# A two-layer hybrid encoder: calls recorded and ordered before they are issued, grouped q, k and v projected with tokens on rows, values 512 wide

## The chip, the cores and the metric

The kernel runs on one core of one Trainium2 chip. The time is device microseconds of one execution; the result is a median of several. Engines: TensorE (PE) multiplies, VectorE (DVE), ScalarE (ACT) and GpSimd (POOL) do the elementwise work, SyncE (SP) issues most transfers.

## The reference

512 tokens of width 1024 in f32 pass two layers. `@` is a matrix product, every norm is an RMS norm, all residuals are plain sums:

```python
h = rms_norm(x, g_mix)
na_q, na_k, na_v, g_q, g_k, g_v = split(h @ w_in)      # 512, 512, 512, 512, 128, 128 columns
a = neighbourhood_attention(na_q, na_k, na_v, rpb)     # 8 heads of 64; 128 queries see 256 keys each here
g_q = rope(rms_norm(g_q per head, q_norm))             # 8 query heads of 64
g_k = rope(rms_norm(g_k per head, k_norm))             # 2 key heads: 4 query heads share one
b = softmax(g_q @ g_k.T / 8) @ g_v                     # all 512 keys, in blocks of 128 queries
x = x + concat(a, b) @ w_out
x = x + memory_attention(rms_norm(x), rms_norm(mem))   # 4 heads of 128 over 256 memory tokens
u = conv3(rms_norm(x) @ w_up)                          # width-3 depthwise over positions
x = x + (silu(gate half of u) * value half of u) @ w_down
```

A last norm follows the second layer.

## The kernel before, in words

**Numbers.** Each f32 operand is split into a high part (`hi`) and a low part (`lo`) of a reduced f32 format. A product is three matmuls, high with high, high with low, low with high (`mm3`), so 1024 rows make 8 x 3 = 24 matmuls per output tile. Only some small jobs (statistics, spreading a row over partitions) are plain f32 matmuls.

**Layout.** Activations are held transposed: `xT` is 8 tiles of 128 features by 512 tokens, and `xg` the split, scaled operand. The projection for neighbourhood attention gives q and k transposed (pairs of heads, 128 rows by 512 tokens) and v with tokens on rows (4 blocks of 128 tokens, twice 256 columns). The grouped projection gives six transposed tiles of 128 x 512: k, q of four head pairs, and v, which is transposed back to tokens on rows.

**Grouped q and k (`gqa_rope`).** VectorE multiplies the tile in two ways with the rotation's table (lines 1147 and 1148), ScalarE squares it (1149), four transfers inside the chip swap its rows for the rotation, matmuls with `pairs` sum the squares over each head's 64 rows, GpSimd takes the power -1/2, matmuls with `ident` spread the result back over the rows, and VectorE multiplies it in (1180) and splits it. `late(n, ...)` holds each of these steps back by some TensorE time.

**Keys doubled.** `split_k` writes a head's key parts on 64 partitions; `double` (line 976) copies them with SP to the other 64, as the score matmul contracts over high and low queries at once.

**Weights.** SP loads each weight block (`raw`, 512 KB, two buffers), ScalarE casts its high part (line 550), GpSimd or VectorE subtracts the low one (551); four buffers of each hold them.

**Attention.** `weave` runs the units of an attention as a pipeline: scores, softmax, transposes of the probabilities, values. Between its steps the `Filler` puts other projection work (the rest of the input projection, then the output projection, memory keys and values) until a quantum of TensorE time is used up (`NA_FILL`, `GQA_FILL`). Neighbourhood attention has 8 units, grouped attention 16 (128 queries of one pair of heads). Probabilities of two query blocks and both heads of the pair share one `xg` tile; there are two such tiles. PSUM has 4 `mm`, 2 `sc` and 2 `tr` buffers.

**Order.** The program is written through `Counted` engines; buffers open in the written order, with priorities from `behind(n)`. At the end `put_in_order` lists the built instructions, prices them with formulas (`busy_and_length`, `HANDOVER`, `BYTES_PER_NS`, `LANDING`), runs them through a planner for six settings (`PLANS`), and fixes the best found order on each engine.

Of the kernel before, what the change touches and what calls it, by code (L numbers as in the profile page):

```python
# [11 lines left out]
F32 = mybir.dt.float32  # L12
# [7 lines left out]
P = 128  # L20
# [20 lines left out]
NA_ORDER = [("q", 0), ("k", 0), ("q", 1), ("k", 1), ("v", 0), ("q", 2), ("k", 2), ("q", 3), ("k", 3), ("v", 1)]  # L41
# [4 lines left out]
GQA_ORDER = ["k", 0, 1, "v", 2, 3]  # L46

NA_FILL = 2550
GQA_FILL = [2300] * 16 + [4300, 3600, 3000, 3000]
# [3 lines left out]
W_BEHIND, N_RAW, N_W, AHEAD, AHEAD_HELD, N_WARM, N_LATE, N_FIRST = 45, 2, 4, 2, 5, 6, 4, (7, 16)  # L53


class InOrder:


    def __init__(self, tc, engine):
        self.tc, self.engine = tc, engine  # L60

    def __getattr__(self, name):
        op = getattr(self.engine, name)
        return op


class Counted(InOrder):


    ns = 0.0  # L70

    def matmul(self, out, lhsT, rhs, **k):
        n = 1
        for d in rhs.shape[1:]:
            n *= d
        self.ns += max(107.0, (n + 32) / 2.4)
        return self.engine.matmul(out, lhsT, rhs, **k)  # L77


class Free:  # L80


    def __init__(self, engine):
        self.engine = engine

    def __getattr__(self, name):
        return getattr(self.engine, name)
# [74 lines left out]
def weave(n, steps, filler, quanta):  # L162
# [12 lines left out]
ENGINES = ["PE", "Activation", "DVE", "Pool", "SP"]  # L175
E_PE, E_ACT, E_DVE, E_POOL, E_SP = range(5)
PLANS = [
    ((60.0, 300.0, 300.0, 300.0, 0.0), 300, given, margin) for given in ((), (E_SP,)) for margin in (0.0, 40.0, 80.0)
]

HANDOVER, BYTES_PER_NS, LANDING = 40.0, 280.0, 2000.0


class Step:


    __slots__ = ("i", "ins", "engine", "busy", "length", "moved", "inside", "shared", "needs", "frees", "opens", "tiles")


def columns(ap):  # L190
    n = 1
    for _, c in ap.ap[1:]:
        n *= c
    return n


def tag_of(tensor):
    return re.sub(r"(_\d+)+$", "", tensor.name)


IN_PSUM = ("mm", "sc", "tr")


def busy_and_length(ins, kind, engine, reads, writes):

    n = max(columns(a) for a in (writes if engine == E_PE else reads + writes))
    if engine == E_PE:
        busy = max(110.0, (n + 32) / 2.4)
        if reads[0].dtype == F32 and not ins.is_transpose:
            busy = 312.0 if n > 64 else 222.0  # L210
        return busy, busy + 170.0
    narrow = min(a.ap[0][1] for a in writes) < P
    if engine == E_ACT:
        busy = 68.0 + 0.805 * n if any(tag_of(a.tensor) in IN_PSUM for a in reads) else 85.0 + 0.855 * n
        busy += 105.0 * (n > 1) * sum(columns(a) == 1 for a in reads) + 93.0 * (len(writes) > 1)
        return busy + 110.0 * narrow, busy + 105.0 + 100.0 * (len(writes) > 1)
    wide = sum(columns(a) > 16 for a in reads)
    if engine == E_DVE:
        if kind == "InstCustomDveAnt":
            return 382.0, 540.0  # L220
        busy = 64.0 + 1.05 * n
        if n <= 16:
            busy = 130.0
        elif kind == "InstTensorScalarPtr":
            busy = 120.0 + 1.05 * n if wide > 1 else 64.0 + 0.78 * n
        return busy + 100.0 * (narrow and n > 16), busy + 85.0
    if kind in ("InstTensorScalarPtr", "InstTensorCopy"):
        busy = 245.0 + 0.82 * n
    else:
        busy = 480.0 + 145.0 * n if n <= 8 else 120.0 + 2.2 * n  # L230
    return busy, busy + 45.0


class Course:


    def __init__(self, tc):
        self.bufs = {tag: m.bufs for p in tc.info.pools for tag, m in p.tag_meta.items()}
        self.steps, self.tag, self.users, self.opened = [], {}, {}, {}
        written, read = {}, {}  # L240
        for ins in tc.nc.cur_bb.bb.instructions:
            kind = type(ins).__name__
            if kind == "BassTilePoolBoundary":
                continue
            s = Step()
            s.i, s.ins, s.engine = len(self.steps), ins, ENGINES.index(str(ins.engine).split(".")[-1])
            s.needs, s.frees, s.opens, s.tiles, s.moved, s.inside = set(), set(), [], [], 0, False
            reads = [x.bass_ap for x in ins.ins if getattr(x, "bass_ap", None) is not None]
            writes = [x.bass_ap for x in ins.outs if getattr(x, "bass_ap", None) is not None]
            if kind == "InstDMACopy":  # L250
                s.busy = s.length = 450.0
                s.moved = 4
                for _, c in writes[0].ap:
                    s.moved *= c
                s.inside = all(type(a.tensor).__name__ == "Tile" for a in reads + writes)
            elif kind == "InstRegisterMove":
                s.busy = s.length = 50.0
            else:
# [1437 lines left out]
```

## Time and profile before

| | |
|---|---|
| median of 3 runs | 1368.02 us (1365.55 to 1368.59) |
| the profiled execution | 1366.98 us, its span 1365.2 |
| PE busy | 1345.2 us (99%), 7068 matmuls |
| DVE busy | 909.3 us (67%) |
| ACT busy | 680.0 us (50%) |
| POOL busy | 695.4 us (51%) |
| transfers | 139.88 MB, mean 102 GB/s |
| mean granted TensorE clock | 0.995 |

The span runs from the first to the last instruction; the time of the execution lies a little above it. An engine's busy time is the sum of what it has in work, so an engine at 99% still says nothing of how well each matmul is used. A group row of the profile gives its line and engine, output and inputs by name, shape and count, then the busy time and mean ns of one, then the idle time just before it with what ended it. The plain f32 matmuls appear twice each, since they take two passes. Roughly, neighbourhood attention of layer 0 ends and the grouped projection runs from 112 to 162 us, grouped attention from there to about 250 us, and the feed-forward network from some 340 us to 686; layer 1 follows in the same way.

### The profile page before, as it was taken

What the parts mean: (1) busy time and instruction counts of PE and PEld (TensorE: products, weight loads), DVE (VectorE), ACT (ScalarE), POOL (GpSimd) and SP (SyncE); (2) the same over time, 40 slices, a digit from 0 to 9 for tenths busy, and PEclk for the clock granted to TensorE, in tenths of its full rate; (3) what the DMA queues carried; (4) which work ended last, traced back from release to release, by engine and by line L of the source; (5) the groups of instructions that cost most, each with busy time, mean ns of one, the idle gap of its engine ahead of it and who ended that gap; (6) DMA issues with size and microseconds to landing.
All of it is one profiled execution on the core that took longest, in us unless ns stands there. A gap on an engine that the chain in (4) does not pass through costs nothing.

```text
span 1365.2 us, 19258 instructions
## 1 busy us (share of the span) xinstructions
PE 1345.2 (99%) x7068; PEld 1154.7 (85%) x7068; DVE 909.3 (67%) x1540; ACT 680.0 (50%) x1258; POOL 695.4 (51%) x493
## 2 busy tenths in 40 slices
PE   9899999999999999999999999999999999999997
PEld 7797889888888888888888988998888888888897
DVE  5567776565897188458546678746759934872884
ACT  5676577564443134234456767755644423432441
POOL 2467656736444444444643676657364444444451
PEclk9999999999999999999999999999999999999999
DMA  6745212322333333332345641133233333323331
GB/s 214 208 135 137 72 39 90 90 82 62 108 100 101 93 94 92 108 93 86 100 146 167 175 116 54 48 94 109 62 93 99 102 93 93 101 84 108 94 91 63
DMA packets 219358, 139.88 MB, mean 102 GB/s; under 512 B 6144, under 2 KB 212224, under 8 KB 219264
## 3 DMA queue, kind: packets, MB, share of 16 engines
q1 hardware_dynamic: 218160, 137.99, 34.4%
q8 instruction: 56, 0.92, 0.3%
q10 hardware_dynamic: 1104, 0.66, 0.2%
q14 instruction: 38, 0.31, 0.1%
HBM read 126.05 MB, written 2.10 MB: 94 GB/s over the span
## 4 chain that ended last, share of the span: by engine, by line
PE 94%; DVE 2%; DMA 1%; ACT 1%; issue 1%; POOL 1%; SPq 0%; ACTq 0%; DVEq 0%; POOLq 0%
PE mm L77 83%; PE sc L77 6%; PE tr L1228 2%; PE tr L77 1%; PE tr L1071 1%; DMA raw<-in_w_in 1%; PE tr L1418 1%; POOL lo L551 0%; DMA t<-t 0%; DVE r L818 0%; DMA par<-in_par 0%; ACT r L984 0%; ACT hi L550 0%; ACT r L966 0%; DVE r L766 0%
## 5 line engine op out<-in xcount | busy, mean ns | idle before, releaser
L551 POOL TENSOR_TENSOR lo<-raw,hi 128x1024 fp32r<-128x1024 f32 (+2 forms) x268 | 504.9, 1894 | 510.2 <-ACT hi L550 510.1
L77 PE MATMUL mm<-xg,hi 128*128 128x512 f32 x1920 | 597.2, 392 | 1.7 <-ACT t L1149 1.7
L77 PEld LDWEIGHTS mm<-xg,hi 128*128 128x128 f32 x1920 | 356.8, 188 | 72.9 <-ACT t L1149 1.9
L550 ACT CAST hi<-raw 128x512 fp32r<-128x512 f32 (+2 forms) x276 | 225.8, 837 | 302.3 <-PE mm L77 232.2
L77 PE MATMUL mm<-xg,lo 128*128 128x512 f32 x960 | 374.5, 390 | 0.0
L77 PE MATMUL mm<-r,hi 128*128 128x512 f32 (+1 forms) x1144 | 332.0, 373 | 0.0
L1519 DVE SCALAR_TENSOR_TENSOR t<-t,par,t 128x504 f32<-128x504 f32 (+1 forms) x352 | 287.7, 859 | 18.7 <-ACT t L1512 15.8
L77 PEld LDWEIGHTS mm<-r,hi 128*128 128x128 f32 x1144 | 207.3, 189 | 35.8
L77 PE MATMUL mm<-r,lo 128*128 128x512 f32 (+1 forms) x572 | 212.8, 372 | 0.0
L77 PEld LDWEIGHTS mm<-xg,lo 128*128 128x128 f32 x960 | 180.7, 188 | 37.9
L77 PEld LDWEIGHTS mm<-r,lo 128*128 128x128 f32 x572 | 107.8, 188 | 18.8
L772 POOL TENSOR_SCALAR t<-t,s 128x512 f32<-128x512 f32 (+1 forms) x112 | 66.7, 611 | 72.8 <-DVE s L1213 39.6
L1504 DVE TENSOR_TENSOR t<-mm,rep 128x512 f32<-128x512 f32 x88 | 60.3, 687 | 62.2 <-PE mm L77 47.0
L1548 DVE TENSOR_TENSOR xT<-xT,mm 128x512 f32<-128x512 f32 x32 | 22.0, 687 | 98.9 <-PE mm L77 98.9
L77 PE MATMUL sc<-r,r 128*128 128x256 f32 (+1 forms) x352 | 72.6, 334 | 0.3 <-DVE r L972 0.3
L1512 ACT ACTIVATE t<-t,par 128x512 f32<-128x512 f32 x88 | 67.5, 807 | 2.9 <-DVE t L1504 2.7
L77 PE MATMUL mm<-r,r 128*128 128x256 f32 (+1 forms) x428 | 64.7, 298 | 3.6 <-DVE r L766 2.6
L1524 ACT CAST r<-t 128x512 fp32r<-128x512 f32 x44 | 27.3, 620 | 78.4 <-DVE t L1522 78.4
L77 PEld LDWEIGHTS mm<-r,r 128*128 128x128 f32 x428 | 57.3, 191 | 6.9 <-DVE r L766 3.2
L1525 DVE TENSOR_TENSOR r<-t,r 128x512 fp32r<-128x512 f32 x44 | 48.1, 1092 | 17.2 <-ACT r L1524 16.5
L77 PEld LDWEIGHTS sc<-r,r 128*128 128x128 f32 x352 | 52.1, 190 | 5.3 <-ACT t L1049 0.4
L1205 DVE TENSOR_REDUCE s<-sc 128x1 f32<-128x512 f32 x64 | 43.5, 686 | 19.0 <-PE sc L77 18.9
(158 smaller groups left out, 1589.0 us busy)
## 6 DMA issues: line engine op xcount, KB each, us to landing
raw<-in_w_up SPq DMA_DIRECT2D x88, 512.0 KB, 3.6
raw<-in_w_in SPq DMA_DIRECT2D x33, 512.0 KB, 4.3
raw<-in_w_down SPq DMA_DIRECT2D x32, 448.0 KB, 3.5
raw<-in_w_mem_kv SPq DMA_DIRECT2D x16, 512.0 KB, 3.5
raw<-in_w_down SPq DMA_DIRECT2D x16, 512.0 KB, 3.8
r<-in_bias SPq DMA_DIRECT2D x16, 384.0 KB, 5.4
r<-r SPq DMA_DIRECT2D x22, 256.0 KB, 5.4
raw<-in_w_out SPq DMA_DIRECT2D x8, 512.0 KB, 3.6
```

The source lines that it names most:

```text
L77: return self.engine.matmul(out, lhsT, rhs, **k)
L550: act.copy(hi[:, k], raw[:, k])
L551: (POOL if eng[0] == "P" else DVE).tensor_sub(lo[:, k], raw[:, k], f(hi)[:, k])
L772: eng.tensor_scalar(e, e, sums[:, col : col + 1], 1.0, op0=ALU.mult, op1=ALU.mult)
L1205: DVE.tensor_reduce(nmx[:, c], sc[j], axis=AX.X, op=ALU.max, negate=True)
L1228: PE.transpose(tr[:, k * P : (k + 1) * P], es[j][:, k * P : (k + 1) * P], ident)
L1504: DVE.tensor_mul(u, us[side], ffn.rep)
L1512: ACT.activation(cc, u, AF.Identity, bias=par[:, l, CB + ch : CB + ch + 1], scale=w[1])
L1519: DVE.scalar_tensor_tensor(cc[:, dst], u[:, src], wi, cc[:, dst], op0=ALU.mult, op1=ALU.add)
L1524: ACT.copy(acts[j][0], cs[0])
L1525: DVE.tensor_sub(acts[j][1], cs[0], f(acts[j][0]))
L1548: DVE.tensor_add(xT[m], xT[m], pm)
```

## The change

**Calls are written down first.** The engines become `Taped` ones: each call makes a `Step` on a `Tape`, with what it reads and writes, and nothing is issued. At the end `Tape.plan` orders all steps with a planner of the same kind, and `play` issues them in that order. Buffers now open in the planned order, not in the written one. `behind` is gone. The planner's constants change (`LANDING` 1450 for 2000, `BYTES_PER_NS` 230 for 280, at most 8 transfers in flight), and transfers inside the chip have no price of their own any more.

**Grouped q, k, v with tokens on rows.** `gqa_project_kv` makes k and v of 128 tokens in one group of 24 matmuls, 256 wide; `gqa_project_q` all 8 heads of 128 tokens in one group of 24 matmuls, 512 wide. The norm is then a sum along a row (`head_norm`), the rotation two products with swapped halves, one product and one sum on VectorE (`turned`), and the result is transposed (4 transposes for k, 16 for q in a layer). k is scaled by its norm on GpSimd; q's norm enters the softmax instead, as a factor of the maximum and as the scale of the exponential (`gr`). The transfers that swapped rows and the matmuls with `pairs` and with `ident` (of a `t` tile) are gone.

**512 wide.** The v of neighbourhood attention and the memory values are projected 512 wide from four weight blocks of 2 x 128 rows (`plan_wide`, `get_wide`). The grouped values take all four query blocks of a pair at once, 512 wide, with one `xg` tile for each head of the pair.

**Smaller things.** `double` and `straddle` are called at once and placed by the planner. A loop before grouped attention finishes all q projections. The filler's quanta are smaller, and more work is done ahead (`N_FIRST`).

The core of the diff:

```diff
-W_BEHIND, N_RAW, N_W, AHEAD, AHEAD_HELD, N_WARM, N_LATE, N_FIRST = 45, 2, 4, 2, 5, 6, 4, (7, 16)
+N_RAW, N_W, AHEAD, AHEAD_HELD, N_WARM, N_LATE, N_FIRST = 2, 4, 2, 5, 6, 4, (12, 22)
...
-NA_FILL = 2550
-GQA_FILL = [2300] * 16 + [4300, 3600, 3000, 3000]
+NA_FILL = 2050
+GQA_FILL = [1850] * 16 + [3450, 2900, 2400, 2400]
...
-HANDOVER, BYTES_PER_NS, LANDING = 40.0, 280.0, 2000.0
+HANDOVER, BYTES_PER_NS, LANDING, IN_FLIGHT = 40.0, 230.0, 1450.0, 8
+ASIDE = {"mm": 1, "r": 9, "t": 9, "s": 9}
+PLANS = [((60.0, 300.0, 300.0, 300.0, 0.0), 300, margin, ASIDE, 3) for margin in (40.0, 80.0, 120.0)]
...
+class Tape:
...
+    def take(self, engine, name, call, args, kwargs):
+        s = Step(len(self.steps), engine, name, call, args, kwargs)
...
+    def play(self, tc):
...
+        for i in self.plan():
+            call, args, kwargs = self.steps[i].call
+            call(*args, **kwargs)
+            while n < len(issued):
+                if type(issued[n]).__name__ != "BassTilePoolBoundary":
+                    if issued[n].engine in last:
+                        tc.add_manual_dep(issued[n], last[issued[n].engine], follows, reason="planned")
+                    last[issued[n].engine] = issued[n].name
+                n += 1
...
@@ split_k
-                late(2, double)
+                double()
...
+        def turned(x, n, which, b, out):
...
+            halves = [slice(0, 32), slice(32, 64)]
+            for d, o in (halves, halves[::-1]):
+                DVE.tensor_mul(at(t2, o), at(x, d), table(1, d))
+            DVE.tensor_mul(x, x, table(0, slice(0, HD)))
+            DVE.tensor_add(out, x, t2)
+
+        def head_norm(x, n, which, b):
...
+            ACT.activation(sq, x, AF.Square)
...
+            DVE.tensor_reduce(view(v), sq, axis=AX.X, op=ALU.add)
...
+            POOL.tensor_tensor(r, v, mhalf[:, :n], op=ALU.pow)
+            return r
...
+        def gqa_project_q():
+
+            w = get_wide("gq")
+            for b in range(NB):
+                pm = ps_mm()
+                bs = slice(b * P, b * P + P)
+                for k in range(KC):
+                    wh, wl = (v[:, k % 2, :] for v in w[k // 2])
+                    mm3(pm, xg[k][0][:, bs], xg[k][1][:, bs], wh, wl, k == 0, k == KC - 1)
...
+                gr[b] = head_norm(x, 8, 0, b)
+                tq = tmp()
+                turned(x, 8, 0, b, tq.rearrange("p (h d) -> p h d", d=HD))
+                late(1.5, lambda b=b, tq=tq: gqa_turn_q(b, tq))
...
@@ gqa_scores
                 DVE.tensor_reduce(nmx[:, c], sc[j], axis=AX.X, op=ALU.max, negate=True)
+                DVE.tensor_mul(nmx[:, c], nmx[:, c], gr[b][:, h])
                 e = tmp()
-                ACT.activation(e, sc[j], AF.Exp, bias=nmx[:, c], accum_out=sums[:, c])
+                ACT.activation(e, sc[j], AF.Exp, bias=nmx[:, c], scale=gr[b][:, h], accum_out=sums[:, c])
...
@@ gqa_transpose_p
-            ib = u % 2
-            if ib == 0:
-                w = xpool.tile([P, KC, S], F32R, tag="xg", name=nm("xg"), bufs=2)
...
+            i, b = divmod(u, NB)
+            if b == 0:
+                ws = [xpool.tile([P, KC, S], F32R, tag="xg", name=nm("xg"), bufs=2) for _ in range(2)]
+                gpt[i] = [w.rearrange("p (n k) q -> p n k q", n=2) for w in ws]
...
@@ gqa_values
-                    PE.matmul(po[:, j], gvt[0][:, k, j, :], pts[j][n][:, k].rearrange("p i n -> p (i n)"),
-                              start=k == 0 and n == 0, stop=k == NB - 1 and n == 1)
+                    PE.matmul(po, gvt[k][:, j, :], gpt[i][j][:, n, k], start=k == 0 and n == 0, stop=k == NB - 1 and n == 1)
...
         weave(8, [(2, na_transpose), None, (1, na_normalise), (0, na_scores), None, (2, na_values), None], attn_fill.run, na_quanta)
+        while None in gq:
+            if attn_fill.closed():
+                late.force()
+            else:
+                attn_fill.step(1)
```

**Where instructions move.** A row of an engine's order has the line (355 for all of the changed kernel, where every call is issued from one place), the operation, output and inputs with buffer numbers, and the shape. Three places of layer 0 follow.

The first is TensorE in the grouped projection. Before, `mm_1619` is a head pair's projection, `mm_1652` and `mm_1660` are values of neighbourhood attention:

```order
L77 MATMUL mm_1619<-xg_133,hi_1437 128x512
L77 MATMUL mm_1619<-xg_132,lo_1438 128x512
L77 MATMUL mm_1646<-ident,t_1472 128x128 x4
L77 MATMUL mm_1652<-r_1586,r_886 128x256
L77 MATMUL mm_1652<-r_1586,r_887 128x256
L77 MATMUL mm_1652<-r_1586,r_885 128x256 x2
L77 MATMUL tr_1673<-pairs,t_1604 128x2 x4
L77 MATMUL mm_1660<-r_1594,r_886 128x256
L77 MATMUL mm_1660<-r_1594,r_887 128x256
L77 MATMUL mm_1660<-r_1594,r_885 128x256 x2
```

And now, in the last block of q (`mm_371`), with a turned block of q (`t_367`) transposed behind it and the output projection (`mm_388`) after:

```order
L355 MATMUL mm_371<-hi_321,xg_98 128x512
L355 MATMUL mm_371<-lo_322,xg_98 128x512
L355 MATMUL mm_371<-hi_321,xg_99 128x512
L355 MATMUL mm_371<-hi_321,xg_98 128x512
L355 MATMUL mm_371<-lo_322,xg_98 128x512
L355 MATMUL mm_371<-hi_321,xg_99 128x512
L355 MATMUL tr_377<-ident,t_367 128x128 x4
L355 MATMUL mm_388<-r_226,hi_379 128x512 x2
L355 MATMUL mm_388<-r_226,lo_380 128x512
L355 MATMUL mm_388<-r_276,hi_379 128x512 x2
```

The groups with `pairs` and with `ident` and a `t` tile into an `mm` tile are not there any more; four transposes of a turned block stand behind its matmuls. VectorE at this place had the two products with the table (L1147, L1148), the product with the spread norm (L1180), and other work:

```order
L1147 SCALAR_TENSOR_TENSOR t_1409<-mm_1320,qkg,r_750 128x512
L1148 SCALAR_TENSOR_TENSOR t_1411<-mm_1320,qkg,r_750 128x512
L1180 TENSOR_TENSOR mm_1432<-t_1259,mm_1432 128x512
L1055 RECIPROCAL s_1392<-s_1392 128x4
L818 SCALAR_TENSOR_TENSOR r_1475<-r_1049,par,r_1475 128x256
L1096 TENSOR_TENSOR t_1415<-mm_1416,t_1415 64x2x128
L1097 TENSOR_TENSOR t_1281<-mm_1416,t_1415 64x256
L1096 TENSOR_TENSOR t_1415<-mm_1424,t_1415 64x2x128
L1097 TENSOR_TENSOR t_1281<-mm_1424,t_1415 64x256
L1159 SCALAR_TENSOR_TENSOR s_1469<-tr_1464,geps 128x8
```

Now it has the sum of squares of a q block (`s_335`), the half products (`t_351`), the full product (`mm_339`) and the sum (`t_350`), with splits of the keys (`r_341`, `r_342`) and of q (`r_353`) among them:

```order
L355 TENSOR_REDUCE s_335<-t_334 128x8
L355 TENSOR_SCALAR s_335<-s_335,geps 128x8
L355 TENSOR_TENSOR r_341<-tr_340,r_341 64x512
L355 TENSOR_TENSOR r_342<-tr_340,r_342 64x512
L355 TENSOR_TENSOR t_344<-mm_345,t_344 64x2x128
L355 TENSOR_TENSOR t_351<-mm_339,r_210 128x8x32 x2
L355 TENSOR_TENSOR r_353<-tr_352,r_353 64x512 x2
L355 SCALAR_TENSOR_TENSOR r_354<-r_255,par,r_354 128x256 x2
L355 TENSOR_TENSOR mm_339<-mm_339,r_210 128x512
L355 TENSOR_TENSOR t_350<-mm_339,t_351 128x512
L355 TENSOR_TENSOR r_356<-tr_355,r_356 128x512
```

The rotation's arithmetic of all four q blocks stands in VectorE's order ahead of the first grouped score.

The second place is TensorE in grouped attention. Before, `mm_2175` and `mm_2285` are values of a pair of heads, 256 wide, each reading one `xg` tile, and `tr` are transposes of probabilities:

```order
L77 MATMUL mm_2175<-xg_2026,r_1631 128x256 x8
L77 MATMUL mm_2193<-r_1502,hi_1833 128x512 x2
L77 MATMUL mm_2193<-r_1502,lo_1834 128x512
L77 MATMUL mm_2193<-r_1722,hi_1833 128x512 x2
L77 MATMUL mm_2193<-r_1722,lo_1834 128x512
L1228 MATMUL tr_2254<-ident,t_2170 128x128 x4
L1228 MATMUL tr_2261<-ident,t_2173 128x128 x4
L77 MATMUL sc_2271<-r_1506,r_1887 128x512 x2
L77 MATMUL sc_2272<-r_1507,r_1887 128x512 x2
L77 MATMUL mm_2285<-xg_2143,r_1631 128x256 x8
```

Now, at the change from the second pair of heads to the third, `mm_523` are the values of the second head of the old pair, and `tr_515` and `tr_516` transposes of the new pair:

```order
L355 MATMUL sc_517<-r_341,r_391 128x512 x2
L355 MATMUL sc_518<-r_342,r_391 128x512 x2
L355 MATMUL tr_515<-ident,t_490 128x128 x4
L355 MATMUL mm_523<-xg_449,r_271 128x512 x8
L355 MATMUL mm_511<-r_329,hi_461 128x256
L355 MATMUL tr_516<-ident,t_491 128x128 x4
L355 MATMUL mm_511<-r_329,hi_461 128x256
L355 MATMUL mm_511<-r_329,lo_462 128x256
```

Values are 512 wide, and the transposes of the new pair stand on both sides of the values that read the old pair's second tile.

The third place is SP around the copies of key pair 2 of neighbourhood attention. Before (`r_695` and `r_696` are the two heads' keys):

```order
L533 DMA raw_707<-in_w_in 128x8x128
L831 DMA t_748<-in_memT 128x2x256
L1357 DMA r_750<-in_rope 128x1024
L533 DMA raw_788<-in_w_in 128x8x128
L976 DMA r_695<-r_695 64x1024
L976 DMA r_696<-r_696 64x1024
L533 DMA raw_874<-in_w_in 128x8x128
L533 DMA raw_882<-in_w_in 128x8x128
```

Now (`r_221` and `r_222`):

```order
L355 DMA r_192<-in_bias 128x768
L355 DMA r_155<-r_152 64x1024
L355 DMA raw_184<-in_w_in 128x4x256
L355 DMA raw_206<-in_w_in 128x4x256
L355 DMA r_221<-r_221 64x1024
L355 DMA r_222<-r_222 64x1024
L355 DMA r_235<-in_bias 128x768
L355 DMA r_236<-in_bias 128x768
```

The copies stood behind the rotation's table and loads of single weight blocks; now they stand behind the two loads for the grouped k and v.

911 lines of the change are left out of this document (426 added, 485 removed).

## The prediction

> **What bounds the kernel now.** I read the page's totals first, then the chain that ended last, then TensorE's waits, and last the stages.
>
> ```profile
> span 1365.2 us, 19258 instructions
> PE 1345.2 (99%) x7068; PEld 1154.7 (85%) x7068; DVE 909.3 (67%) x1540; ACT 680.0 (50%) x1258; POOL 695.4 (51%) x493
> PE 94%; DVE 2%; DMA 1%; ACT 1%; issue 1%; POOL 1%; SPq 0%; ACTq 0%; DVEq 0%; POOLq 0%
> ```
>
> TensorE is busy 99% of the span and 94% of the chain runs through it. What the change does to TensorE's own work is therefore paid nearly in full, and a wait of TensorE is paid in full. The wait table is short; its four rows that touch the changed code are:
>
> ```profile
> PE mm L77 <- DVE r L766: 2.6, 2, 1.6
> PE mm L77 <- ACT t L1149: 1.7, 1, 1.7
> PE mm L77 <- DVE r L986: 1.6, 2, 1.0
> PE tr L77 <- DVE r L766: 0.8, 1, 0.8
> ```
>
> The stages in which the change sits, one row each (the end of neighbourhood attention with the grouped projections, layer 0; the grouped attention, layer 0; the memory queries' start, where VectorE is fullest; the grouped attention, layer 1):
>
> ```profile
> core 0: us, PE busy (x) PEld busy (x) DVE busy (x) ACT busy (x) POOL busy (x), PEclk, DMA share, GB/s
> 112.00:162.00 50.00, 47.32 (x268) 40.67 (x267) 37.72 (x72) 27.80 (x63) 35.97 (x33) 0.97 0.31 89
> 162.00:230.00 68.00, 68.00 (x464) 62.29 (x464) 52.60 (x102) 53.95 (x126) 45.06 (x52) 1.00 0.19 59
> 344.00:400.00 56.00, 56.00 (x248) 46.35 (x248) 52.53 (x68) 27.66 (x35) 25.39 (x11) 1.00 0.35 104
> 812.00:890.00 78.00, 78.00 (x504) 70.04 (x503) 60.81 (x115) 59.27 (x134) 53.59 (x59) 1.00 0.22 65
> ```
>
> In grouped attention TensorE loses nothing, while VectorE is at 77% (52.60 of 68) and 78%, and ScalarE at 79% (53.95 of 68). In 344 to 400 us VectorE is at 94% and TensorE still loses nothing. The granted clock is 1.00, so there is no clock to win back.
>
> **The matmuls' prices** come from unbroken pieces of the chain, whose starts are one matmul apart (a single record's mean is longer, since records overlap). The second fence is another stretch of that view:
>
> ```profile
> 343.99 342.76 PE mm L77 x1512
> 1345.44 10.09 PE mm L77 x84
> ```
>
> ```profile
> 178.92 0.88 PE tr L1228 x8
> ...
> 343.10 0.89 PE tr L77 x8
> ```
>
> A 512-wide matmul takes 342.76 / 1512 = 0.2267 us, a 256-wide one 10.09 / 84 = 0.1201, a 128-wide transpose 0.88 / 8 = 0.11. Four matmuls in plain f32 (two passes each, so eight records) take 0.89.
>
> ```profile
> L77 PE MATMUL mm<-hi,xg 128*128 128x256 f32 x256 | 48.8, 284 | 0.6 <-DVE r L986 0.6
> L77 PE MATMUL mm<-lo,xg 128*128 128x256 f32 x128 | 36.2, 283 | 0.0
> L77 PE MATMUL mm<-xg,r 128*128 128x256 f32 x256 | 36.3, 283 | 0.0
> L77 PE MATMUL mm<-hi,r 128*128 128x256 f32 x128 | 24.5, 283 | 0.0
> L77 PE MATMUL mm<-lo,r 128*128 128x256 f32 x64 | 18.1, 283 | 0.0
> L77 PE MATMUL mm<-ident,t 128*128 128x128 f32 x80 | 10.5, 274 | 0.0
> L77 PE MATMUL tr<-pairs,t 128*128 128x2 f32 x80 | 9.6, 241 | 0.8 <-DVE r L766 0.8
> ```
>
> **Wider tiles: -4.3 us.** The first five rows are the matmuls that become 512 wide: v (256 + 128), the grouped values (256), memory values (128 + 64), together 832, which become 416. The grouped k and v go the other way: 288 matmuls of 512 for all grouped projections become 192 of 512 (q) and 192 of 256 (k with v). Net, 640 matmuls of 256 go and 320 of 512 come: -640 x 0.1201 + 320 x 0.2267 = -76.9 + 72.5 = -4.3. The gain is that 256 columns cost 0.1201, more than half of 0.2267. On this the Trainium skill (TensorE: Matmul & The Clock Gate, Back-to-back issue gap) speaks against the change: its isolated warm gap, columns / 2.4 plus 2.5 ns, makes 109 and 216 ns, by which widening would save 0.8 us instead of 4.3. The trace disagrees with it at both widths, and its rows decide.
>
> **Matmuls that go: -14.3 us.** The last two rows are the norm of the grouped heads: in ten units (q in four, k in one, two layers) four matmuls with `pairs` and four with `ident`, 80 records each. Twenty groups at 0.89 make -17.8; the narrow `pairs` group may be a little cheaper, though its weights are as large. New are 40 transposes of rotated q and k, and 8 of v go: 32 x 0.11 = +3.5. Net -14.3. With the widening TensorE's work falls by **18.6 us**.
>
> **Waits that go: -2.5 us.** The L1149 row and the last row of the wait table hang on the rotation that is removed (1.7 + 0.8). It could be none, if another wait comes up in their place.
>
> **The tiles of the wide values: +6.8 us.** A pair of grouped heads now fills both `xg` tiles, one a head, where one tile in two was free before. So the first evictions of the next pair wait until the values have read the old tile.
>
> ```profile
> L765 ACT CAST xg<-tr 128x512 fp32r<-128x512 f32 x64 | 34.7, 590 | 13.6 <-PE tr L1228 12.8 <-ACT r L768 0.3
> L766 DVE TENSOR_TENSOR xg<-tr,xg 128x512 fp32r<-128x512 f32 x64 | 43.2, 683 | 4.4 <-ACT xg L765 4.3
> ```
>
> An eviction takes 0.59 + 0.68 = 1.27, and only then are the two `tr` buffers free for the next transposes. In the new order of layer 0 the transposes that need the second head's buffer follow the second head's values by 0.45, 0.12 and 0 us of other TensorE work at the three changes of pair: 0.8 + 1.15 + 1.3 with the handovers is 3.3 to 3.4 a layer, 6.8 in both (layer 1 has the same order there). Ends: 0, if handovers are already in what I add up, and 13, if ScalarE, which stands at the waiting cast in its order, is late for the exponentials behind it by as much again.
>
> **VectorE: +1 us more.** This is the term that I had to choose. The durations:
>
> ```profile
> L1043 DVE CUSTOM_DVE_ANT_0 sc<-sc,r 128x256 f32<-128x256 f32 x64 | 26.9, 438 | 8.6 <-PE sc L77 7.5
> L1043 DVE DVE_READ_ACCUMULATOR2_ANT s<- 128x1 f32 x64 | 9.0, 140 | 0.0
> L1097 DVE TENSOR_TENSOR t<-mm,t 64x256 f32<-64x256 f32 x32 | 13.3, 417 | 1.3
> L818 DVE SCALAR_TENSOR_TENSOR r<-r,par,r 128x256 fp32r<-128x256 f32 x16 | 12.4, 800 | 0.3 <-DMA t<-t 0.2
> L986 DVE TENSOR_TENSOR r<-mm,r 64x512 fp32r<-64x512 f32 x28 | 19.3, 689 | 4.9 <-ACT r L984 4.4
> L1205 DVE TENSOR_REDUCE s<-sc 128x1 f32<-128x512 f32 x64 | 43.5, 686 | 19.0 <-PE sc L77 18.9
> L772 DVE TENSOR_SCALAR s<-s,s 128x1 f32<-128x1 f32 x32 | 5.3, 207 | 0.4
> ```
>
> All grouped q must now be turned before the first grouped score, so VectorE's turning is crowded into the end of neighbourhood attention. In the new order of layer 0, from the eviction of key pair 3 to the sum of the last turned q, VectorE has 111 instructions: 12 score passes with their reads (12 x 0.578 = 6.9), 20 adds of 256 (8.3), 8 memory operands at 0.800 (6.4), 14 splits at 0.689 (9.6), for q 8 full-width products and sums (5.5), 8 half products at 0.417 (3.3) and 3 sums of squares (2.1), and 26 others, each at the row of its width (8.6): 50.7 us. Over the same places TensorE has 51.6 us by the prices above. In grouped attention, from the first score to the 28th, VectorE has 28 maxima (19.2), 28 new one-column products with q's norm (5.8), 36 full-width steps (24.8), and 4.2 of small ones: 54.0 us beside 58.4 of TensorE. Summed durations overlap: for the same 28 scores before, they give 55.6 of TensorE's 68.1, 82%, where the window shows 77%. Scaled by 0.94, the two stretches need 47.6 and 50.8, together 98.4 of 110 us, a share of 89%.
>
> So a layer loses 98.4 / share - 110: nothing at 89% and less than the 94% shown once, 17.8 at the 77% that attention reaches now. With the 3.4 us that the value tiles add, the share is 98.4 / 113.4 = 87%, nearer to the 94% than to the 77%, which was no limit, since TensorE lost nothing there; so I add little, 1 us in all, which also covers ScalarE (its exponentials get a second column). Ends: 0 and 2 x (17.8 - 3.4) = 29.
>
> **Doubled keys: +4 us.** The copies of k's halves are now planned by a shorter landing time.
>
> ```profile
> L957 DVE TENSOR_TENSOR mm<-mm,rep 128x512 f32<-128x512 f32 x6 | 4.2, 693 | 1.4 <-PE mm L77 1.3
> L966 ACT CAST r<-mm 64x512 fp32r<-64x512 f32 x16 | 9.3, 581 | 0.5 <-DVE mm L957 0.3
> DMA to landing us min/median/max: 3.0/5.4/8.7
> ```
>
> From a key projection's last matmul to its first score, the old order left TensorE 14 to 26 us of other work. The new one leaves 9.2 and 8.8 us for pairs 2 and 3 of layer 0, 10.2 and 8.0 in layer 1 (pair 2 of layer 0: 30 matmuls of 512, 13 of 256, 8 transposes). The chain is 0.69 + 0.58 + 0.69 + 5.4 = 7.4 by the median landing: no wait. By the longest, 8.7, it is 10.7, and 6.6 us are missing in the four together. I take 4; ends 0 and 6.6.
>
> **The sum.** -18.6 - 2.5 + 6.8 + 1 + 4 = -9.3. The profiled execution took 1366.98 us (span 1365.2 and 1.8 around it), so it becomes 1357.7; the median of the three runs shown is 1.0 above it: **1359 us**. Edits at nothing: weight loads, casts and subtractions keep their bytes and hide under TensorE as before; SP loses the 40 copies of the rotation and gets the straddling copies of v and the table earlier, with room between (DMA share 0.31 at most in these stages). Where that cover goes, the price is VectorE's or the keys' above.
>
> **The rivals.**
> - **All of it is won.** Tiles, VectorE and keys cost nothing that shows. For it: no loss at 94%. Against it: that stage has few handovers. -18.6 - 2.5 + 0 to 4 gives 1347 to 1351. Chance 0.13.
> - **The gain is eaten.** VectorE holds 84.5% (12.9 over two layers, the tiles in it) and the copies cost 6.6: -18.6 - 2.5 + 12.9 + 6.6 = -1.6, 1366; with neighbours 1363 to 1370. Chance 0.12.
> - **VectorE becomes the bound.** The place is the end of neighbourhood attention and grouped attention in both layers. If VectorE can be used there no better than its present 77%, because each step in turn waits for TensorE and ScalarE, the price is 2 x 17.8 = 35.6 and the time 1368 - 21.1 + 4 + 35.6 = 1387. It decides from where 2 x (98.4 / share - 110) exceeds 17.1 + 2.7, a share of 82%. For it: 112 to 162 us, where TensorE already lost 2.7 with VectorE at 75% (37.72 of 50). Chance 0.18.
>
> That the change does not do what it says is excluded by the orders: the `pairs` and `ident` groups are gone and the widths are there.
>
> **How the numbers follow.** The forecast case has the other 0.57, and by itself spans 1353 to 1364. Within 0.2% of before (1365.3 to 1370.8), about what a measurement of this kernel can tell from no change, lies some 0.07, from the second and third rivals. Faster: 0.57 + 0.13 and half of the second rival, 0.76. Slower: 0.17. The range, 1347 to 1374, holds the forecast, the first two rivals and the nearer part of the third.
>
> **What would show it.** In the changed profile TensorE's matmul work should be about 18.6 us less, with no `pairs` group; the wait for the rotation gone; VectorE at 85 to 90% before and in grouped attention; three waits of about 1 us a layer of transposes for an eviction, each behind a second head's values; and short waits for r before the first scores of pairs 2 and 3. The forecast is wrong if TensorE's waits for VectorE or ScalarE reach 15 us, or if the 512-wide matmuls are not near 0.227 us.

## The result and the profile after

| | before | changed |
|---|---|---|
| median | 1367.22 us (1365.55 to 1368.59, 4 runs) | 1353.58 us (1352.78 to 1354.90, 4 runs) |
| span of the profiled execution | 1365.2 us | 1353.1 us |
| PE busy | 1345.2 us | 1332.5 us |
| DVE busy | 909.3 us | 941.4 us |
| PE matmul records | 7068 | 6620 |

The ratio is 0.9902 (0.9885 to 0.9919): 13.4 us faster. The forecast was 9.0 us faster, 1359, and the measured time lies in its range. But the sum came near partly by luck: four of its terms are far off, and their errors nearly cancel.

The page of the changed kernel, its totals and its chain by engine:

```profile
span 1353.1 us, 18192 instructions
PE 1332.5 (98%) x6620; PEld 1120.9 (83%) x6620; DVE 941.4 (70%) x1609; ACT 679.6 (50%) x1230; POOL 686.5 (51%) x475
PE 88%; DVE 8%; ACT 2%; DMA 1%; issue 1%; POOL 0%; ACTq 0%; DVEq 0%
```

TensorE has fewer instructions, but VectorE's part of the chain went from 2% to 8%: it holds TensorE up now. The wait table names the place, scores that wait for ScalarE:

```profile
PE sc L355 <- ACT t L355: 4.8, 10, 1.4
PE sc L355 <- ACT xg L355: 2.1, 2, 1.6
PE tr L355 <- DVE r L355: 1.6, 1, 1.6
...
PE tr L355 <- DVE xg L355: 0.3, 1, 0.3
PE tr L355 <- POOL t L355: 0.3, 1, 0.3
PE sc L355 <- DMA r<-r: 0.2, 1, 0.2
```

The rotation's waits are gone. There is one new kind of wait of weight, the first row. The waits of transposes for `xg`, forecast at 6.8 us, are 0.3, and that of scores for the doubled keys (`r<-r`), forecast at 4, is 0.2.

The stages that answer to those before (the end of neighbourhood attention, then grouped attention, of layer 0; the start of the feed-forward network, which the prediction calls the memory queries' start; grouped attention of layer 1):

```profile
95.00:146.00 51.00, 49.42 (x293) 42.90 (x292) 46.80 (x103) 33.66 (x78) 31.17 (x30) 1.00 0.24 74
146.00:216.00 70.00, 66.94 (x383) 54.68 (x382) 61.77 (x122) 54.34 (x118) 47.02 (x51) 1.00 0.22 68
332.00:388.00 56.00, 56.00 (x249) 46.34 (x248) 53.27 (x69) 28.31 (x36) 25.41 (x10) 1.00 0.33 95
809.00:880.00 71.00, 67.97 (x382) 55.76 (x381) 61.45 (x122) 54.23 (x118) 46.75 (x51) 0.98 0.22 67
```

VectorE is at 92% (46.80 of 51), 88% (61.77 of 70) and 87%, about the forecast 85 to 90%. But grouped attention, in which TensorE lost nothing before, loses 3.1 us here and 3.0 in layer 1.

Where the time came from is read from one long piece of the chain, the feed-forward network of each layer. First before (that of layer 0, at 343.99, is shown in the prediction), then the changed kernel:

```profile
1008.79 330.29 PE mm L77 x1554
```

```profile
332.06 342.76 PE mm L355 x1512
996.12 293.58 PE mm L355 x1295
```

Up to layer 0's piece the changed kernel gains 343.99 - 332.06 = 11.9 us, from there to layer 1's 664.80 - 664.06 = 0.7, and after it nothing (356.4 and 357.0). Both layers lost the same matmuls. So in layer 1 new waits ate nearly all of it, while layer 0 gained something besides.

### The profile page after: what moved, and what is told of

It reads as the page before. It is cut to its first block, busy times and chain, and to the rows that moved or that the text cites. A ratio compares the mean times of both kernels' runs of the same rounds, so it can differ in the third digit from the quotient of the medians.

```text
span 1353.1 us, 18192 instructions
## 1 busy us (share of the span) xinstructions
PE 1332.5 (98%) x6620; PEld 1120.9 (83%) x6620; DVE 941.4 (70%) x1609; ACT 679.6 (50%) x1230; POOL 686.5 (51%) x475
## 4 chain that ended last, share of the span: by engine, by line
PE 88%; DVE 8%; ACT 2%; DMA 1%; issue 1%; POOL 0%; ACTq 0%; DVEq 0%
PE mm L355 79%; PE sc L355 5%; PE tr L355 4%; DVE s L355 3%; DVE t L355 2%; DVE r L355 1%; ACT t L355 1%; DVE xg L355 1%; DMA r<-r 0%; DVE xT L355 0%; ACT r L355 0%; DMA par<-in_par 0%; DVE sc L355 0%; DVE mm L355 0%; ACT xg L355 0%
## 5 line engine op out<-in xcount | busy, mean ns | idle before, releaser
L355 PE MATMUL mm<-xg,hi 128*128 128x512 f32 x1728 | 535.1, 390 | 0.0
L355 ACT CAST hi<-raw 128x512 fp32r<-128x512 f32 (+3 forms) x281 | 228.4, 831 | 313.4 <-PE mm L355 282.5
L355 DVE SCALAR_TENSOR_TENSOR t<-t,par,t 128x504 f32<-128x504 f32 (+1 forms) x352 | 247.7, 739 | 35.9 <-ACT t L355 32.2
L355 DVE TENSOR_TENSOR xT<-xT,mm 128x512 f32<-128x512 f32 (+1 forms) x64 | 39.4, 618 | 118.3 <-PE mm L355 118.2
L355 PE MATMUL mm<-hi,xg 128*128 128x512 f32 (+1 forms) x384 | 107.9, 357 | 0.0
L355 ACT ACTIVATE t<-sc,s,s 128x512 f32<-128x512 f32 (+1 forms) x96 | 67.9, 709 | 41.5 <-DVE s L355 41.2
L355 DVE TENSOR_TENSOR t<-t,t 128x512 f32<-128x512 f32 (+1 forms) x68 | 76.4, 1123 | 8.6 <-ACT t L355 4.4
L355 DVE TENSOR_TENSOR r<-t,r 128x512 fp32r<-128x512 f32 (+1 forms) x52 | 71.5, 1375 | 13.5 <-ACT r L355 12.5
L355 PEld LDWEIGHTS mm<-hi,xg 128*128 128x128 f32 x384 | 68.6, 189 | 9.4
L355 PE MATMUL tr<-ident,t 128*128 128x128 f32 x488 | 70.8, 274 | 3.1 <-DVE r L355 1.6
```

Source lines behind the costliest of these rows:

```text
L355: call(*args, **kwargs)
```

## The experiments

The theory after this reading: in layer 0 the recorded order took early waits away; in both layers a new wait in grouped attention, through VectorE's small product of the maximum with q's norm, ate most of what the matmuls gave back. The rivals are the prediction's own: VectorE is simply too crowded, or the wide values' tiles hold the transposes.

The small product is the suspect because of its durations. VectorE's group of it, and one of the long ones with the GpSimd instruction beside it and the exponential behind it (the timelines of VectorE, GpSimd, ScalarE and TensorE, changed kernel):

```profile
L355 DVE TENSOR_TENSOR s<-s,s 128x1 f32<-128x1 f32 x64 | 30.9, 483 | 1.8
```

```profile
146.24 0.16 DVE L355 TENSOR_TENSOR s<-s,s 128x1 f32<-128x1 f32 x1
...
149.45 1.30 DVE L355 TENSOR_TENSOR s<-s,s 128x1 f32<-128x1 f32 x1
...
149.45 2.50 POOL L355 TENSOR_TENSOR lo<-raw,hi 128x512 fp32r<-128x512 f32 x2
...
150.78 0.78 ACT L355 ACTIVATE t<-sc,s,s 128x512 f32<-128x512 f32 x1 [2.44 <-DVE s L355]
...
151.71 0.73 PE L355 MATMUL sc<-r,r 128*128 128x512 f32 x2 [1.35 <-ACT t L355]
```

The product of one column that began at 146.24 took 0.16 us, the one at 149.45 took 1.30. This one began with a GpSimd subtraction (two in 2.50, so 1.25 each) and ended with it. Then the exponential ran, which frees the score buffer, and then TensorE's next scores, 1.35 late.

It is no single case. Of the 64 products 26 took over 0.4 us, and each of these ended within 0.02 us behind the end of a GpSimd instruction (24 tensor-tensor, 2 tensor-scalar). But not every GpSimd instruction holds one: the short product at 146.24 ran inside a GpSimd power of 8 columns.

```profile
145.33 1.63 POOL L355 TENSOR_TENSOR s<-s,mhalf 128x8 f32<-128x8 f32 x1
```

**1. The product in scalar form.** The same arithmetic, with the norm as a per-partition scalar (`normalise` issues one tensor-scalar instruction: times that column, then times 1.0):

```diff
-                DVE.tensor_mul(nmx[:, c], nmx[:, c], gr[b][:, h])
+                normalise(nmx[:, c], gr[b], 2 * i + j)
```

Expected: 

> The product of the maximum with q's norm is issued as a tensor-scalar instruction (the norm as a per-partition scalar) in place of a tensor-tensor one; every engine's order stays the same. In the changed kernel these 64 products took 0.483 us on average, most 0.16 but a third of them 0.5 to 1.30, ending where a GpSimd tensor-tensor instruction ends. Port theory (VectorE's instruction with two SBUF inputs is held while GpSimd has the memory port, and the held product delays the exponential behind it, which holds the score buffer that TensorE waits for): the mean falls to 0.16 to 0.21, TensorE's waits of scores for ScalarE (4.8 us) mostly go, the time falls by 4 to 9 us, to 1345 to 1350. Rival, crowding (VectorE and ScalarE have too much work in grouped attention, whatever holds one product): the products get shorter, but the time stays within 2 us of the changed kernel's 1353.6. Rival, held all the same (this form is held too): the mean stays near 0.48 and the time at 1353.6.

Measured: 1343.03 us, ratio to the kernel before on its chip 0.9845 (0.9821 to 0.9870). The product's group (with 32 others that were of this form already) and TensorE's waits on ScalarE and VectorE in this kernel:

```profile
L355 DVE TENSOR_SCALAR s<-s,s 128x1 f32<-128x1 f32 x96 | 19.1, 211 | 2.3
```

```profile
PE sc L355 <- ACT xg L355: 1.8, 1, 1.8
PE tr L355 <- DVE r L355: 1.5, 1, 1.5
...
PE tr L355 <- DVE t L355: 0.9, 2, 0.5
...
PE sc L355 <- ACT t L355: 0.6, 2, 0.3
```

The mean falls from 0.483 to 0.211 and the wait of scores for the exponential from 4.8 to 0.6. None of the 96 took more than 0.217, although 40 of them ran wholly inside a GpSimd subtraction. Every instruction kept its place, so this one form is worth 8 to 11 us (0.9902 and, in experiment 5, 0.9918 against 0.9845; 1353.6 and 1354.3 against 1343.0), at the theory's upper end or above. That is twice the wait shown: the rest of it lay in matmuls counted as busy (PE busy falls by 6.8 us with the same matmuls). By an estimate, 1.7 us of these 6.8 are the granted clock's. In the changed kernel it stood at half for 3.4 us right behind the waits of layer 1's first grouped scores (1.35 and 0.32 us, at 814.54 and 815.83), and two 512-wide matmuls take 1.05 us there, 0.62 a little later; here it is 1.00 through grouped attention of both layers (changed kernel, then this one):

```profile
816.70:820.10 3.40, 3.40 (x12) 2.72 (x11) 3.31 (x5) 2.45 (x6) 2.78 (x4) 0.50 0.39 113
```

```profile
146.00:210.00 64.00, 63.60 (x379) 54.60 (x378) 55.24 (x122) 53.40 (x116) 45.88 (x50) 1.00 0.25 74
803.00:867.00 64.00, 63.61 (x378) 54.27 (x377) 55.14 (x123) 53.39 (x117) 45.80 (x51) 1.00 0.26 75
```

Whether the waits bring that stretch on was not tested; the like waits of layer 0 have none behind them. Crowding as the main cause falls: the same list of work, less only the held time, runs without the loss, with VectorE still at 86% (55.24 of 64). The layers now gain alike. Pieces of the chain before and behind grouped attention of each layer, first the changed kernel, then this one:

```profile
131.19 5.53 PE mm L355 x24
794.07 5.49 PE mm L355 x24
```

```profile
130.18 5.49 PE mm L355 x24
325.98 342.76 PE mm L355 x1512
787.99 5.49 PE mm L355 x24
983.76 293.58 PE mm L355 x1295
```

Layer 0 is 6.1 us shorter than in the changed kernel (325.98 against 332.06), of which 1.0 lies ahead of grouped attention (130.18 against 131.19). Layer 1 is 6.3 shorter (657.78 against 664.06), all of it in grouped attention, since the gain at its start is still 6.1 (787.99 against 794.07). The 12.6 us between the two spans thus hold 1.0 that has nothing to do with the product.

**2. q scaled before its transposes.** The product and the second column of the exponential go:

```diff
+                heads = tq.rearrange("p (h d) -> p h d", d=HD)
+                POOL.tensor_mul(heads, heads, gr[b].unsqueeze(2).to_broadcast([P, 8, HD]))
...
-                DVE.tensor_mul(nmx[:, c], nmx[:, c], gr[b][:, h])
...
-                ACT.activation(e, sc[j], AF.Exp, bias=nmx[:, c], scale=gr[b][:, h], accum_out=sums[:, c])
+                ACT.activation(e, sc[j], AF.Exp, bias=nmx[:, c], accum_out=sums[:, c])
```

Expected: 

> q is multiplied by its norm on GpSimd right after its rotation (8 products 512 wide), so that the 64 products of the maximum and the second column of the 64 exponentials go; the planner makes a new order. Port theory: 64 x 0.483 = 31 us of VectorE and 64 x 0.09 = 6 us of ScalarE go from grouped attention, at the price of 8 GpSimd products of about 1.3 us before it; 1344 to 1350. Crowding: the same sign, since VectorE's share falls too, so this run tells only together with the first: if the first stays at 1353.6 and this one gains, it is crowding. Tile theory (the wide values' tiles hold the transposes): no change, 1352 to 1355.

Measured: 1343.73 us, 0.9848 (0.9827 to 0.9869). No product at all is no better than an unheld one: 12 us less of VectorE's work (928.9 to 917.0) and 6 less of ScalarE's (679.1 to 673.1) bring nothing that shows. The order is new here and GpSimd has 8 products more, so a small gain could be hidden; but what the first experiment won needs no more than the hold.

**3. Grouped values 256 wide.** The old tiles, one for two query blocks and both heads:

```diff
-            if b == 0:
-                ws = [xpool.tile([P, KC, S], F32R, tag="xg", name=nm("xg"), bufs=2) for _ in range(2)]
+            ib = u % 2
+            if ib == 0:
+                w = xpool.tile([P, KC, S], F32R, tag="xg", name=nm("xg"), bufs=2)
...
```

Expected: 

> The grouped values go back to 256 wide, one xg tile for two query blocks of both heads, all else as in the changed kernel; the planner makes a new order. Tile theory, the term of the prediction (6.8 us of waits, because the next pair's evictions wait for the values): matmuls cost 256 x 0.1201 - 128 x 0.2267 = +1.7, the waits go, 1353.6 + 1.7 - 6.8 = 1348.5. Rival (the tiles cost nothing, the loss in grouped attention is elsewhere): +1.7, 1355.3. Above 1357 the old way of the values would have waits of its own here.

Measured: 1348.37 us, 0.9883 (0.9862 to 0.9904). That is the tile theory's number, 1348.5, but it need not be its cause. The planner's order is new, and with it the product is held less (mean 0.388 for 0.483):

```profile
L355 DVE TENSOR_TENSOR s<-s,s 128x1 f32<-128x1 f32 x64 | 24.8, 388 | 1.2
```

So this run alone is inconclusive, and the next pair settles it.

**6. Both: scalar form and values 256 wide.** The edit is that of the first and of the third together.

Expected: 

> Scalar form of the product (as the first experiment, 1343.0) and grouped values 256 wide with the old tiles; every engine's order is that of the experiment with 256-wide values and the held product, 1348.4. Tile theory (the wide values' tiles cost up to 6.8): 1343 + 1.7 - 6.8 = 1338 to 1341. No cost of tiles, wide values gain their matmul time: 1343 + 1.7 = 1344.7. Port theory for the pair with equal order: 1348.4 minus 3 to 5.

Measured: 1342.64 us, 0.9835 (0.9820 to 0.9849), against 1343.03 with wide values. In the same order the held product was worth 5.7 us here (1348.37; the profiles' orders differ in nothing but its form), and the tiles cost nothing like 6.8: both kinds come out alike within what is measured. Nor do the wide values' 1.7 us of matmuls show; that some 2 us for the tiles eat them up is not excluded.

**4. The tape alone.** The kernel before, all its arithmetic and widths, with the changed kernel's recording, planner and issue:

```diff
-    PE, SP = Counted(tc, nc.tensor), InOrder(tc, nc.sync)
+    tape = Tape()
+    PE, ACT, DVE, POOL, SP = (
+        Taped(tape, e, calls) for e, calls in zip(ENGINES, (nc.tensor, nc.scalar, nc.vector, nc.gpsimd, nc.sync)))
...
+    tape.play(tc)
...
-        put_in_order(tc)
```

Expected: 

> The kernel before with all its arithmetic, widths and filler quanta, but its calls recorded, planned and issued as in the changed kernel (the late steps keep their place in the written order, which is only the planner's start). The matmul work is that of before. Arithmetic theory (the prediction: 18.6 us of matmuls gone, little from the order): 1364 to 1368. Order theory (the tape takes away the early waits of layer 0, some 7 us between 20 and 160 us, and the arithmetic's gain was mostly eaten by new waits): 1358 to 1362. That the tape is all of it: 1354.

Measured: 1355.07 us, 0.9935 (0.9913 to 0.9956): 9 us, two thirds of the whole gain, without any of the arithmetic. The profile has TensorE's whole wait table at

```profile
PE sc L357 <- ACT xg L357: 2.0, 2, 1.6
PE tr L357 <- POOL ident masks.py:199: 1.3, 1, 1.3
PE tr L357 <- POOL s L357: 1.0, 1, 1.0
PE tr L357 <- ACT t L357: 0.7, 1, 0.7
PE mm L357 <- POOL lo L357: 0.5, 1, 0.5
PE mm L357 <- ACT t L357: 0.5, 1, 0.5
```

of which the first four are the start and the end. All waits for r and the rotation in layer 0 are gone or at 0.5. The layers:

```profile
332.08 342.76 PE mm L357 x1512
996.65 293.58 PE mm L357 x1295
```

Layer 0's piece begins at 332.08, as in the changed kernel; layer 1 takes 664.57, as before. So in the changed kernel the tape's gain stands in layer 0, and what the arithmetic took away the held product gave back in each layer.

**5. The changed kernel again**, as a reference on another chip, with no edit.

Expected: 

> The changed kernel once more, unchanged, beside the next three on the same chip, since the kernel before took 1364 and 1367 us on two chips: 0.990 of the kernel before within 0.002, by every theory.

Measured: 1354.31 us, 0.9918 (0.9901 to 0.9934), as the first time.

**7. v and memory values 256 wide, scalar form.** Weight blocks of 4 x 128 rows by 256 for those of 2 x 128 by 512:

```diff
-                plan_wide("v", w_in, 1024, "DPDP")
+                for g in range(2):
+                    for kh in range(2):
+                        cols(("v", g, kh), w_in, 4 * kh, 4, 1024 + 256 * g, 256, "DP"[kh])
...
-                pm = ps_mm()
+                    pm = ps_mm()[:, :256]
```

Expected: 

> Scalar form of the product, and v and the memory values projected 256 wide from weight blocks of 4 x 128 rows by 256 (as in the kernel before), all else as in the changed kernel; new order. 576 matmuls of 256 in place of 288 of 512. By the trace's prices (0.1201 and 0.2267): 69.2 - 65.3 = +3.9, 1347. By gaps of columns / 2.4 plus 2.5 ns (109 and 216): +0.6, 1343.6, as if width were worth nothing.

Measured: 1349.56 us, 0.9887 (0.9873 to 0.9902), 6.5 us above the first experiment (span 1347.2 against 1340.5, 6.7). The row of its wait table that stood at 0.6 there is

```profile
PE sc L355 <- ACT t L355: 3.3, 2, 2.1
```

The first grouped scores wait 2.7 us longer in this order. The other 4.0 fit the matmuls, 3.9 by the trace's prices and 0.6 by the formula that the prediction cites; TensorE's busy time agrees, with 4.3 us more (1330.0 against 1325.7). Since the order is new, the split into 2.7 and 4.0 is a reading of the rows, not a measurement of the width alone.

**8. The tape alone with a held product.** The reverse of the first: one product by ones for each grouped maximum, in the old arithmetic.

```diff
                 DVE.tensor_reduce(nmx[:, c], sc[j], axis=AX.X, op=ALU.max, negate=True)
+                DVE.tensor_mul(nmx[:, c], nmx[:, c], ones)
```

Expected: 

> The tape-alone kernel (1355.1) with one tensor-tensor product more per maximum in grouped attention: the maximum times a column of ones, 64 in all, which changes no value. Port theory: as in the changed kernel the product is held (mean 0.4 to 0.5 us) and delays the exponential; +4 to +10, 1359 to 1365. Crowding alone: 64 x 0.16 = 10 us more of VectorE work at 77%, which was no limit; within 1.5 us of 1355.

Measured: 1358.86 us, 0.9952 (0.9937 to 0.9967), against 1355.07 and 0.9935; the spans are 1358.1 and 1353.3. The product:

```profile
L357 DVE TENSOR_TENSOR s<-s,ones 128x1 f32<-128x1 f32 x64 | 22.2, 348 | 0.7
```

It is held here too. It costs 3.8 us by the medians, 4.8 by the spans and 2.3 by the ratios: at the low end of the port theory's 4 to 10 or under it, and above the 1.5 of crowding. The ratios' intervals overlap, so this run by itself is a weak witness. The product is held less than in the changed kernel (0.348 for 0.483); why it also costs less in the old arithmetic was not tested.

**9. The kernel before with the new transfer constants**, and **10. the tape alone with the old ones:**

```diff
-HANDOVER, BYTES_PER_NS, LANDING = 40.0, 280.0, 2000.0
+HANDOVER, BYTES_PER_NS, LANDING = 40.0, 230.0, 1450.0
...
-    ((60.0, 300.0, 300.0, 300.0, 0.0), 300, given, margin) for given in ((), (E_SP,)) for margin in (0.0, 40.0, 80.0)
+    ((60.0, 300.0, 300.0, 300.0, 0.0), 300, given, margin) for given in ((), (E_SP,)) for margin in (40.0, 80.0, 120.0)
```

```diff
-HANDOVER, BYTES_PER_NS, LANDING, IN_FLIGHT = 40.0, 230.0, 1450.0, 8
+HANDOVER, BYTES_PER_NS, LANDING, IN_FLIGHT = 40.0, 280.0, 2000.0, 8
```

Expected of 9: 

> The kernel before with its own way of ordering (buffers open as written, priorities, late steps), but the planner's transfer constants and margins of the changed kernel (LANDING 1450, BYTES_PER_NS 230, margins 40, 80, 120; transfers inside the chip keep their own price). The tape alone took the span from 1365.2 to 1353.3, all of it in layer 0 (11.9 us). If the constants do it, this kernel comes to 1353 to 1358 and layer 0 ends near 332 us. If buffers opening in the planned order do it, it stays at 1362 to 1368 and layer 0 ends near 344.

Expected of 10: 

> The tape-alone kernel with the old transfer constants (LANDING 2000, BYTES_PER_NS 280), margins and the rest as on the tape. If the opening of buffers does it: 1353 to 1357, layer 0 ends within 2 us of 332. If the constants do it: 1360 to 1366, layer 0 ends near 340 or later.

Measured: 1363.53 us, 0.9988 (0.9977 to 0.9999), and 1358.87 us, 0.9947 (0.9932 to 0.9962). Their pieces of the chain, of 9 (both layers) and of 10 (layer 0):

```profile
337.99 342.76 PE mm L77 x1512
1004.80 304.69 PE mm L77 x1344
```

```profile
334.50 342.76 PE mm L357 x1512
```

The constants alone give 1.6 us of the tape's 9; the tape without them gives 6.3 on this chip. By the time, then, most of it comes with the recording. But neither run lies clearly where one theory had it. 10's time is between the 1353 to 1357 of the one and the 1360 to 1366 of the other. The constants alone bring layer 0's piece forward by 6.0 us against the profile of before (343.99), and layer 1 loses 2.0 of them again (666.81 for 664.80); the tape without the constants brings it forward by 9.5. What in the recording does it is not shown: buffers that open in the planned order are one candidate, but the new planner also has other settings, a limit on transfers in flight and no price of its own for transfers inside the chip. What the constants add to the tape (0.9947 to 0.9935) can't be told from nothing.

## Why the prediction was right, and where it was not

The prices of the matmuls and the work that goes were right by their mechanism. That the sum came within some 4 us of the measured gain is in good part luck: the arithmetic's 12.0 us less the held product's 8 to 11 leave 1 to 4, and the tape, of which I had priced next to nothing, gave 9.0. Term by term:

- **Wider tiles, -4.3.** The prices fit where they were tried: 4.0 for the widths of v and memory values, against 3.9 (experiment 7, in a new order). For the grouped values no gain was found (experiment 6), where the prices say 1.7; that stays open.
- **Matmuls that go, -14.3.** Taken with the widening, -18.6 was forecast. From the tape alone to the scalar form, the measured step is 12.0 us by the medians and 12.8 by the spans, and the waits of the second are 2.0 us longer in the rows shown (1.5 + 0.9 + 0.6 against 0.5 + 0.5). So some 15 of 18.6 are found, and TensorE's busy time says the same (1340.6 to 1325.7, 14.9 less); the values' 1.7 are part of what is missing, and about 2 us stay open. That a plain f32 matmul takes two passes is read from its two records in the profile.
- **Waits that go, -2.5.** Right in kind, mis-sized: I counted only the two waits that hang on the rotation. Recording the calls took away nearly all the waits of layer 0 ahead of grouped attention, 9.0 us by the medians and 11.9 between the profiles (the profiled execution of before lies 3 us above that kernel's median on the tape's chip, and has a stretch of 3.4 us at half the clock behind its wait at 146.33). The step that failed is that I priced what the new arithmetic needs, and took the new way of ordering as free of effect on the waits elsewhere.
- **Tiles of the wide values, +6.8.** Wrong. I took it that the two `tr` buffers alternate. TensorE's timeline of the first experiment, at the same change of pair (8 matmuls of values, one of 256, then the transposes):

```profile
188.55 0.60 PE L355 MATMUL tr<-ident,t 128*128 128x128 f32 x4
188.90 2.09 PE L355 MATMUL mm<-xg,r 128*128 128x512 f32 x8
190.83 0.28 PE L355 MATMUL mm<-r,hi 128*128 128x256 f32 x1
190.95 0.60 PE L355 MATMUL tr<-ident,t 128*128 128x128 f32 x4
```

  The transposes at 190.95 follow the values with no wait, where I had 1.15. The tape gave them the buffer that the transposes at 188.55 had left, not the one that was held by the old tile. The held eviction does exist; it is the first of these two on ScalarE, and it began at 191.19, behind the values and when the transposes were already running:

```profile
191.19 1.08 ACT L355 CAST xg<-tr 128x512 fp32r<-128x512 f32 x2
```

  So the eviction waited for the tile as I said, but TensorE did not wait for the eviction.
- **VectorE, +1.** The shares were right (87 to 92%), their meaning was not. At those shares the scalar form loses next to nothing (0.4 us of 64 in grouped attention of each layer, experiment 1); the loss came from one small instruction, which I priced at 0.207 from a tensor-scalar row of the same size, though the diff issues a tensor-tensor one with both inputs in SBUF. It measured 0.483 and cost 8 to 11 us. The planner has the same blind spot: it marks a VectorE instruction as sharing the port with GpSimd only when two inputs are over 16 columns wide. The Trainium skill (SBUF — State Buffer, SBUF: two separate sides) says that VectorE and GpSimd share one port pair, that an instruction of VectorE with two SBUF inputs needs it against a GpSimd one that reads SBUF, and that who starts first has it to the end. The timeline at 149.45, the ends of the 26 long products and the drop from 0.483 to 0.211 with the form alone agree with that; experiment 8 does so weakly. The product at 146.24, short inside a GpSimd power whose operands lie in SBUF, does not.
- **Keys, +4.** 0.2. I took landings between before's median, 5.4 us, and its longest, 8.7. In the changed kernel the copies land sooner, in 3.6 at the median by its page.
- **The rivals.** VectorE did become what TensorE waits for, but not by its share, and it cost less than a third of the 35.6 that the rival had. That all is won (1347 to 1351) did not come true, but the scalar form alone brings the kernel below it. All that stands beside the matmuls' 18.6 was forecast at +9.3 and is +6.5 by the profiles (the span fell by 12.1): -11.9 for the tape, +12.6 for the hold and the 1.0 ahead of it (1353.1 - 1340.5), and the 5.8 by which the arithmetic's 12.8 falls short of 18.6. These are single executions; by the medians the tape is worth 9.0 and the hold 8 to 11.
- **The signs.** VectorE's shares and the 0.2267 us of a 512-wide matmul came as said. TensorE's work fell by 12.7 us instead of 18.6, and the waits for tiles and keys did not come (0.3 and 0.2). Its waits for VectorE and ScalarE stayed under the 15 us that I had named, though the hold cost 8 to 11, since more than half of that is not in the wait table.

The best version run is the scalar form, 1343.03 us (with the values 256 wide, 1342.64 is no different).

## What to carry to other kernels

Look at the longest of a group beside its mean: a one-column instruction that sometimes takes eight times its usual time is waiting inside, and no row of idle time says so. On a path between scores and exponentials, try the form that needs one SBUF tensor and a per-partition scalar; here it was never held. And where a change brings a new order with new arithmetic, run the order alone: here it was two thirds of the gain, and most of the arithmetic's own gain was hidden by a single line.

## What the runs showed of the hardware that I had not expected

- A VectorE product of two SBUF columns took 0.15 to 1.30 us, with the 26 long ones (over 0.4) ending within 0.02 us of a GpSimd instruction's end; the scalar form of the same product took 0.20 to 0.22, in the same order.
- A hold inside VectorE is not seen as a wait of VectorE: it counts as busy. VectorE's busy time grew by 32 us in all; 20.7 of them (64 x (0.483 - 0.16)) are the held products.
- TensorE's busy time hides waits as well: with the same matmuls it is 1332.5 us in the changed kernel and 1325.7 in the scalar form. An estimated 1.7 of the difference is a stretch of 3.4 us at half the granted clock, behind two waits of 1.35 and 0.32 us; what the rest is made of, the profile does not resolve.
